# Weight blocks in one transfer each, and chunk 0 multiplied block by block

## The chip, the cores and the metric

The kernel runs on one core of a Trainium2 chip. The metric is the device time of one execution in microseconds (us); the time before is the median of three runs. A profile of one execution, with the time of every instruction and every DMA packet, goes with it. The engines are called PE (TensorE, the matrix products), DVE (VectorE), ACT (ScalarE), POOL (GpSimd) and SP (SyncE, which here issues stores); PEld is the loading of weights into TensorE.

## The reference

```python
# x: 16 x 512 x 1024, weight: 1024 x 768, both float32
y = np.matmul(x, weight)
mean = np.mean(y, axis=(0, 1), keepdims=True)
var = np.var(y, axis=(0, 1), keepdims=True)
y_norm = (y - mean) / np.sqrt(var + eps)
return (gamma * y_norm + beta).astype(np.float32)
```

A product of 8192 x 1024 with 1024 x 768, and a normalization of each of the 768 columns over all 8192 rows. No element of the output can be written before the last row of its column has been multiplied.

## The kernel before

**Tiles.** The 8192 rows of x are cut into 16 chunks of 512 rows. The 1024 elements of the inner dimension are cut into 4 blocks (`JW = 4`, index `jw`) of 256; each block is two steps (`e` = 0, 1) of 128, the partitions of TensorE. The 768 columns are six tiles of 128. Columns 0 to 255 (`NA`) are computed as rows (output rows on the partitions; `rows_unit`, `mm_rows`, line 493), the four tiles from column 256 on as columns (output columns on the partitions; `col_unit`, `mm`, line 558).

**Loads.** Both x and w are read as float32 and turned to bfloat16 by the DMA, all on GpSimd's queue. `w_sb` holds w as 128 partitions x 4 blocks x 2 x 768. Partition 32 i + c holds, for block jw, the two rows 2 (32 (4 i + jw) + c) and the next, 1536 elements that lie together in memory. One call of `load_w(jw, jw1)` (line 378) loads the blocks from jw up to jw1, in four transfers of 32 partitions, one for each i. `load_x` (line 386) also makes four transfers of 32 partitions. The order of the loads (line 426) is: x0 (rows 0 to 255 of chunk 0), block 0 of w, x1 (the other half of chunk 0), block 1, blocks 2 and 3 together, x2 and x3 (the halves of chunk 1), then chunks 2, 3 and on (line 392 issues all of x, line 383 all of w). VectorE turns each half chunk so that the inner dimension comes on the partitions (`turn_x`; line 421, for chunks 2, 3 and 6 line 414).

**The queue's lanes.** A transfer on GpSimd's queue gets one of eight semaphores in turn, so the issue of a transfer waits until the one eight places ahead of it has landed. The planner knows this as `LANES = 8`.

**The order of the work.** Every piece of work is a `Task` with a priority, a planned duration on one or several engines, and what it depends on. `arrange` is a planner that runs when the kernel is built: it takes again and again the engine that can begin first, and gives it the task of best priority among those that can begin within 0.2 us (`LOOK`) of the earliest. Its model of the DMA (`Wires`) uses fixed rates. The order that comes out is kept on each engine; on the chip, an engine that waits for something keeps everything behind it waiting. The turns of x have the best priority on VectorE (-1000 and up).

**Chunk 0 on TensorE.** Idle matmuls (`wake`, 16 on a zero tile and 22 small ones; lines 574 and 577) fill the time up to the arrival of data. Then come, by `part(q0, q1, jws)`: the first half of chunk 0 with block 0, a filler of four idle matmuls (`FILL`, 2 of `wake`), the second half with block 0, both halves with block 1. Then both halves with blocks 2 and 3: the rows (two units), and the four column tiles. Each of the six results of chunk 0 gathers in its own PSUM bank over all four blocks. When the rows of a half are done, ScalarE squares them (line 642), VectorE adds them to the running sums (line 645), GpSimd or VectorE adds the squares (line 649), and ScalarE keeps a copy (line 655). When a column tile is done, VectorE takes its statistics (line 694) and ScalarE keeps a copy (line 698). Chunk 1 begins after that, in two halves, with x2 and x3.

The rest of the kernel multiplies the other chunks, takes the statistics of one group of columns after the other, and normalizes, turns and stores a group while the next is multiplied.

Of the kernel before, what the change touches and what calls it, by code (L numbers as in the profile page):

```python
# [227 lines left out]
def kernel(  # L228
# [9 lines left out]
    nc = tc.nc  # L238
# [10 lines left out]
    NT = N // P  # L249
# [14 lines left out]
    GA = 2  # L264
# [26 lines left out]
    def seq(bi):  # L291

        ins = bi.ins
        prev = last.get(ins.engine)
        if prev is not None:
            tc.add_manual_dep(
                ins, prev,
                mybir.DependencyInfo(mybir.DependencyClass.NoSync, mybir.DependencyReason.DATA),
                reason="order",
            )  # L300
        last[ins.engine] = ins.name
        return bi
# [48 lines left out]
    def task(prio, engines, emit, deps=(), lock=False, **kw):  # L351
        t = Task(prio, engines, emit, deps, **kw)
        t.lock = lock
        tasks.append(t)
        return t

    def dve(occ):
        return {"DVE": (occ, occ + 0.09)}

    def act(occ):  # L360
        return {"ACT": (occ, occ + 0.11)}
# [14 lines left out]
    w_ready, x_ready, x_slot, plain, last_loads = {}, {}, {}, {}, []  # L376

    def load_w(jw, jw1):
        def emit(eng):
            rows = weight.rearrange("(i jw c e) n -> i c jw (e n)", i=4, jw=JW, e=2)  # L380
            dst = w_sb.rearrange("p jw e n -> p jw (e n)")
            for i in range(4):
                seq(nc.gpsimd.dma_start(dst[32 * i:32 * i + 32, jw:jw1], rows[i, :, jw:jw1]))
        return emit

    def load_x(m0, rows, slot):
        def emit(eng):
            x_bf = piece(slot).bitcast(bf16).rearrange("p (t k) -> p t k", k=KQ)
            slot.tile = x_bf
            src = x_flat[m0:m0 + rows].rearrange("(t r) k -> r t k", r=32)  # L390
            for i in range(4):
                bi = seq(nc.gpsimd.dma_start(x_bf[32 * i:32 * i + 32], src[:, :, KQ * i:KQ * (i + 1)]))  # L392
            slot.loader.ins = bi.ins
        return emit
# [8 lines left out]
    def turn_x(xslot, slot, m0, t0, jw0, jw1, new, rows=QR):  # L403
        def emit(eng):
            single = m0 // CH in SINGLE
            if new:
                xT_sb = xtpool.tile([P, JW, 2, CH] if single else [P, JW, CH, 2], bf16, tag="xT")
                slot.tile = xT_sb
            half, row = divmod((m0 + 32 * t0) % CH, QR)
            if single:  # L410
                src = xslot.tile[:, t0:t0 + rows // 32].rearrange("p t (jw c e) -> p t jw e c", jw=JW, e=2)
                dst = slot.tile[:, :, :, half * QR + row:half * QR + row + rows]
                dst = dst.rearrange("p jw e (t r) -> p t jw e r", r=32)
                seq(nc.vector.transpose(dst[:, :, jw0:jw1], src[:, :, jw0:jw1]))  # L414
                return
            src = xslot.tile[:, t0:t0 + rows // 32].rearrange("p t k -> p (t k)").bitcast(f32)
            src = src.rearrange("p (t jw c) -> p t jw c", jw=JW, c=32)
            dst = slot.tile.rearrange("p jw m e -> p (jw m e)").bitcast(f32)
            dst = dst.rearrange("p (jw q t r) -> p q t jw r", jw=JW, q=QPC, r=32)
            dst = dst[:, half, row // 32:(row + rows) // 32, jw0:jw1]  # L420
            seq(nc.vector.transpose(dst, src[:, :, jw0:jw1]))  # L421
        return emit

    for c in range(C):
        x_slot[c] = Slot(xts)
    order = [("x", 0), ("w", 0, 1)] + [("x", 1), ("w", 1, 2), ("w", 2, 4)]
    order += [("x", q) for q in range(2, SHORT * QPC)] + [("c", c) for c in range(SHORT, C - 1)]
    at = M - CH
    for rows in (CH-P,P):
# [2 lines left out]
    t = 1.0  # L432
    affine = None
    for kind, n, *n1 in order:
        if kind == "w":
            took = 4 * 192 * 4 * (n1[0] - n) / 4 * PER_KB * 1.024
            w_ready[n] = task(t, {"POOL": (2.0, 2.0)}, load_w(n, *n1), dma=took)
            w_ready[n].count = 4
            t += 2.1 * (n1[0] - n)
            if n1[0] == JW:  # L440
                idt = task(t, {"POOL": (0.6, 0.6)}, lambda eng: make_identity(nc, ident))
                task(t, act(0.25), lambda eng: seq(nc.scalar.copy(ident32, ident)), [idt])
            continue
        rows = n1[0] if kind == "p" else QR if kind == "x" else CH
        m0 = n if kind == "p" else n * rows
        if m0 == M // 2:
            affine = task(t, {"SP": (5.0, 7.0)}, load_affine, [x_ready[m0 // CH - 3, 0, JW]])
        slot = Slot(rings, rows // 32 * KQ // 2)
        load = task(
            t, {"POOL": (2.68 * rows / CH, 2.68 * rows / CH)}, load_x(m0, rows, slot), dma=rows * K * 4 / 1024 * PER_KB * 1.024,  # L450
            takes=[slot])
        load.count = 4
        slot.loader = load
        last_loads.append(load)
        t += 2.7 * rows / QR
        for i in range(rows // QR):
            c, q = divmod(m0 // QR + i, QPC)
            for j0, j1 in ((0, JW // 2), (JW // 2, JW)) if m0 < CH else ((0, JW),):
                new = q == 0 and j0 == 0
                x_ready[c, q, j1] = task(  # L460
                    -1000 + t, dve((2.2 if c in SINGLE else 1.16) * (j1 - j0) / JW + 0.02),
                    turn_x(slot, x_slot[c], m0, i * QR // 32, j0, j1, new), [load],
                    uses=[slot] if new else [slot, x_slot[c]], takes=[x_slot[c]] if new else [])
                if not new:
                    x_ready[c, q, j1].deps.append(x_ready[c, 0, JW // 2 if m0 < CH else JW])
            x_ready.setdefault((c, q, JW // 2), x_ready[c, q, JW])
        if rows % QR:
            t0 = rows // QR * QR // 32
            m1 = m0 + 32 * t0
            c, q = divmod(m1 // QR, QPC)  # L470
            x_ready["tile", m1 // P] = task(
                -1000 + t, dve(0.63), turn_x(slot, x_slot[c], m0, t0, 0, JW, False, P),
                [load, x_ready[c, 0, JW]], uses=[slot, x_slot[c]])
            x_ready[c, q, JW] = x_ready[c, q, JW // 2] = x_ready["tile", m1 // P]
# [123 lines left out]
    def rows_unit(c, ts, jws=range(JW)):  # L598
        key = "row", c, ts[0]
        slot = bank_of.setdefault(key, None) or Slot(banks)  # L600
        bank_of[key] = slot
        kw = {"takes": [slot], "uses": [x_slot[c]]} if jws[0] == 0 else {"uses": [slot, x_slot[c]]}
        h = ts[0] * P // QR
        t = pe_task(0.873 * len(ts) * len(jws) / JW, mm_rows(c, ts, list(jws), slot),
                    waits(jws, c, h, h + 1), key, **kw)
        if jws[-1] == JW - 1:
            rows_stats(c, ts, slot, t)
        return t

    def col_unit(nt, c, jws, q0=0, q1=QPC):  # L610
        slot = bank_of.setdefault((nt, c), None) or Slot(banks)
        bank_of[nt, c] = slot
        first = jws[0] == 0 and q0 == 0
        xs = [plain[c][0][jw] for jw in jws] if c in plain else [x_slot[c]]
        kw = {"takes": [slot], "uses": xs} if first else {"uses": [slot] + xs}
        t = pe_task((1.728 if c in plain or c in SINGLE else 1.808) * len(jws) / JW * (q1 - q0) / QPC,
                    mm(nt, c, list(jws), slot, q0, q1),
                    waits(jws, c, q0, q1) + ([plain[c][1][jw] for jw in jws] if c in plain else []), (nt, c), **kw)
        if q1 - q0 == QPC:
            t.hosts = 4  # L620
        if jws[-1] == JW - 1 and q1 == QPC:
            col_stats(nt, c, slot, t)
        return t
# [133 lines left out]
    def part(q0, q1, jws):  # L757
        for h in range(q0, q1):
            rows_unit(0, [2 * h, 2 * h + 1], jws)
        for nt in range(GA, NT):  # L760
            col_unit(nt, 0, jws, q0, q1)
# [3 lines left out]
    pe_task(0.87 * FILL, wake(FILL, fill_slot), [w_ready[0]], takes=[fill_slot])  # L765
    part(1, 2, [0])
    part(0, 2, [1])
    for h in range(2):
        rows_unit(0, [2 * h, 2 * h + 1], [2, 3])
    for nt in range(GA, NT):  # L770
        col_unit(nt, 0, [2, 3])

    halves = [range(JW // 2), range(JW // 2, JW)]
    merges = []
# [455 lines left out]
    nt = NT - 1  # L1230
# [40 lines left out]
    for c, r0, rows in ends:  # L1271
        due = E + 2.0 + 0.6 * c
        n = max(rows // CH, 1)
# [30 lines left out]
    order = arrange(tasks, turns)  # L1304
# [39 lines left out]
```

## Time and profile before

| | |
|---|---|
| median of 3 runs | 207.76 us (207.47 to 208.3) |
| span of the profiled execution, first to last instruction | 206.5 us |
| time of the profiled execution itself | not given by the page; the median is 1.26 us above the span |
| TensorE busy | 191.4 us, 93% of the span |
| VectorE, ScalarE, GpSimd busy | 76%, 68%, 64% |
| granted clock of TensorE, mean | 0.985 of full speed |
| DMA moved | 48.73 MB, of which 18.36 MB by GpSimd's queue |
| issue of one transfer of w on GpSimd | 0.51 us, 12 of them |

How to read it: times in the views are counted from the start of the span. A line of a timeline gives start, length, engine, source line, operation, what is written and what is read, and how many instructions are drawn together; in brackets stands how long the engine had been idle and what released it. A line of the waits gives who waited for whom, the sum in us, the number of waits and the longest. A line of a table of windows gives the stretch, its length, the busy time of PE, PEld, DVE, ACT and POOL, the granted clock, the DMA engines' share, and GB/s (counted in bytes written, so that a load that halves its bytes counts half). The DMA issues give KB of each transfer and the median time from issue to landing.

### The profile page before, as it was taken

Reading aid. Unit: us, or ns where it says so; the run is one execution under the profiler, and the core shown is the slowest. Engines: PE = TensorE matmul, PEld = TensorE weight load, DVE = VectorE, ACT = ScalarE, POOL = GpSimd, SP = SyncE. Lnnn points to the kernel's source line nnn. Section 1 sums busy time; section 2 is a strip of 40 time slices with the busy share of each in tenths; the row PEclk is TensorE's granted clock in tenths of the full one; section 3 lists DMA queues with packets and bytes.
Section 4 is the critical chain, followed back from the end, with each engine's and each line's share of the span. In section 5 each row is a group of like instructions: output and inputs, shape, how many; then the busy total and the mean of one; then the engine's idle time right before and its main releaser. Section 6 shows DMA issues by size and latency. Waiting matters only on the chain.

```text
span 206.5 us, 3506 instructions
## 1 busy us (share of the span) xinstructions
PE 191.4 (93%) x1211; PEld 116.3 (56%) x1226; DVE 156.3 (76%) x238; ACT 139.8 (68%) x248; POOL 132.0 (64%) x148
## 2 busy tenths in 40 slices
PE   7998999999999999999999999999999999996900
PEld 3465564747488888777875444444444445553600
DVE  4220779999999999968989998977999648947900
ACT  2000560369989999998978767997376776866950
POOL 7877964877488999999304999599954440440000
PEclk9999999999999999999999999999999999999995
DMA  5999999999999999999676898999999999999898
GB/s 55 169 168 193 192 196 196 196 198 197 190 193 197 197 197 195 196 197 195 110 120 199 311 339 307 267 350 307 315 317 245 291 325 308 274 341 347 254 347 243
DMA packets 98497, 48.73 MB, mean 236 GB/s; under 512 B 24240, under 2 KB 97968, under 8 KB 98480
## 3 DMA queue, kind: packets, MB, share of 16 engines
q0 software_dynamic: 34688, 18.36, 65.1%
q1 hardware_dynamic: 63792, 30.16, 52.8%
q8 instruction: 9, 0.15, 0.3%
q14 instruction: 8, 0.07, 0.1%
HBM read 36.71 MB, written 25.17 MB: 300 GB/s over the span
## 4 chain that ended last, share of the span: by engine, by line
PE 82%; DMA 8%; ACT 3%; issue 1%; POOL 1%; DVE 1%; ACTq 0%; POOLq 0%
PE y_ps L558 51%; PE y_ps L493 23%; DMA ring<-in_x_dram 5%; PE y_ps L798 4%; ACT o_sb L1293 3%; DMA w_sb<-in_weight_dram 3%; PE o_ps L1028 2%; PE a_ps L887 1%; POOL ring L392 1%; PE y_ps L736 1%; PE o_ps L1058 0%; ACTq L1339 0%; PE tot_ps L855 0%; DVE fin L743 0%; ACT y_sb L746 0%
## 5 line engine op out<-in xcount | busy, mean ns | idle before, releaser
L558 PEld LDWEIGHTS <-w_sb 128*128 128x128 bf16 x512 | 49.7, 97 | 57.4
L558 PE MATMUL y_ps<-x_pl,w_sb 128*128 128x512 bf16 x256 | 60.5, 379 | 0.3
L392 POOL DMA_DIRECT2D ring<-in_x_dram x76 | 47.5, 630 | 13.0 <-DVE xT_sb L414 5.0
L558 PE MATMUL y_ps<-xT_sb,w_sb 128*128 128x512 bf16 (+1 forms) x241 | 55.1, 376 | 0.4
L493 PE MATMUL y_ps<-w_sb,xT_sb 128*128 128x256 bf16 x448 | 50.7, 273 | 0.6 <-DMA w_sb<-in_weight_dram 0.6
L493 PEld LDWEIGHTS <-xT_sb 128*128 128x128 bf16 x448 | 43.6, 98 | 8.3 <-issue 1.7
L421 DVE STREAM_TRANSPOSE xT_sb<-ring 128x1024 f32<-128x1024 f32 (+1 forms) x29 | 31.2, 1111 | 12.4 <-DMA ring<-in_x_dram 12.2
L694 DVE BATCH_NORM_STATS2 stats<-y_ps 128x6 f32<-128x512 f32 x46 | 30.9, 687 | 12.7 <-PE y_ps L558 12.5
L698 ACT CAST y_sb<-y_ps 128x512 bf16<-128x512 f32 x51 | 29.4, 590 | 14.5 <-DVE stats L694 12.4
L926 POOL TENSOR_TENSOR ring<-ring,sum 128x1024 f32<-128x1024 f32 (+1 forms) x11 | 23.7, 2193 | 14.6 <-DVE ring L921 14.5
L649 POOL TENSOR_TENSOR sum<-sum,sq_sb 128x512 f32<-128x512 f32 x21 | 26.9, 1281 | 3.2 <-ACT sq_sb L642 2.1
L642 ACT ACTIVATE sq_sb<-y_ps 128x512 f32<-128x512 f32 x28 | 16.3, 607 | 18.0 <-PE y_ps L493 17.1
L645 DVE TENSOR_TENSOR sum<-y_ps,sum 128x512 f32<-128x512 f32 x28 | 18.9, 675 | 9.1 <-ACT sq_sb L642 7.8
L530 ACT COPY x_pl<-xT_sb 128x1024 bf16<-128x1024 bf16 x24 | 24.4, 1052 | 1.7 <-DVE xT_sb L421 1.7
L655 ACT CAST y_sb<-y_ps 128x512 bf16<-128x512 f32 x28 | 16.0, 599 | 7.8 <-DVE sum L645 7.6
L530 POOL COPY x_pl<-xT_sb 128x1024 bf16<-128x1024 bf16 x15 | 16.1, 1108 | 8.0 <-DVE x_pl L530 5.2
L921 DVE TENSOR_TENSOR ring<-y_sb,a_ps 128x1024 f32<-128x1024 bf16 (+1 forms) x16 | 16.7, 1080 | 0.3 <-DMA out_dram<-ring 0.3
L1139 POOL TENSOR_TENSOR ring<-ring,sum 128x1024 f32<-128x1024 f32 x4 | 9.6, 2412 | 11.0 <-DVE ring L1135 11.0
L1193 ACT CAST ring<-ring 128x1024 f32<-128x1024 bf16 x15 | 15.7, 1049 | 1.0 <-DMA ring<-y_sb 1.0
L1028 PE MATMUL o_ps<-ident,y_sb 128*128 128x128 bf16 x104 | 14.2, 221 | 2.2 <-DVE y_sb L1280 2.0
L414 DVE STREAM_TRANSPOSE xT_sb<-ring 128x2048 bf16<-128x2048 bf16 x6 | 13.5, 2289 | 0.2 <-DMA ring<-in_x_dram 0.2
L574 PE MATMUL idle_ps<-idle_sb 128*128 128x512 f32 x20 | 11.2, 717 | 1.5 <-DVE idle_sb L314 1.5
(97 smaller groups left out, 155.0 us busy)
## 6 DMA issues: line engine op xcount, KB each, us to landing
out_dram<-ring SPq DMA_DIRECT2D x38, 512.0 KB, 3.7
ring<-in_x_dram POOLq DMA_DIRECT2D x52, 256.0 KB, 8.8
out_dram<-o_sb SPq DMA_DIRECT2D x6, 512.0 KB, 4.9
ring<-in_x_dram POOLq DMA_DIRECT2D x16, 128.0 KB, 5.3
out_dram<-ring SPq DMA_DIRECT2D x4, 256.0 KB, 3.0
w_sb<-in_weight_dram POOLq DMA_DIRECT2D x8, 96.0 KB, 5.1
w_sb<-in_weight_dram POOLq DMA_DIRECT2D x4, 192.0 KB, 5.9
ring<-in_x_dram POOLq DMA_DIRECT2D x4, 192.0 KB, 8.1
```

The source lines that it names most:

```text
L392: bi = seq(nc.gpsimd.dma_start(x_bf[32 * i:32 * i + 32], src[:, :, KQ * i:KQ * (i + 1)]))
L421: seq(nc.vector.transpose(dst, src[:, :, jw0:jw1]))
L493: seq(nc.tensor.matmul(y_ps[:, s], x_of(c, jw, e, t * P, (t + 1) * P), w_sb[:, jw, e, 0:NA], start=(s == 0 and jw == 0 and e == 0), stop=( ...
L530: seq(nc.scalar.copy(dst, pairs) if eng == "ACT" else ENG[eng].tensor_copy(dst, pairs))
L558: seq(nc.tensor.matmul(y_ps, w_sb[:, jw, e, nt * P:(nt + 1) * P], moving(c, jw, e, q0 * QR, q1 * QR, parted), start=(jw == 0 and e == 0 an ...
L645: seq(nc.vector.tensor_add(sum1, slot.tile[:, 0:n], sum1))
L649: seq(ENG[eng].tensor_add(acc, acc, state["sq"][:, 0:n]))
L694: seq(nc.vector.bn_stats(dst, slot.tile))
L698: seq(nc.scalar.copy(y(nt, c), slot.tile))
L921: seq(nc.vector.tensor_mul(slot.o, y_row[c].y[:, s0:s1], aff[0][:, None, :].to_broadcast([P, n, NA])))
L926: seq(ENG[eng].tensor_add(slot.o, slot.o, row[:, None, :].to_broadcast([P, n, NA])))
L1028: seq(nc.tensor.transpose(dst, src, ident))
```

## The change

`load_w` makes one transfer for each block over all 128 partitions, instead of four for 32 partitions each. Blocks 2 and 3 are loaded and waited for one by one, and chunk 0 is multiplied first by block 2 and then by block 3, by the same `part` that does block 1, instead of by both in each unit. The planner's figures for GpSimd's time of a load of w and for the number of its transfers change with that: 0.6 us and one transfer for each block, instead of 2.0 us and four for each call.

```diff
 def load_w(jw, jw1):
     def emit(eng):
         rows = weight.rearrange("(i jw c e) n -> i c jw (e n)", i=4, jw=JW, e=2)
         dst = w_sb.rearrange("p jw e n -> p jw (e n)")
-        for i in range(4):
-            seq(nc.gpsimd.dma_start(dst[32 * i:32 * i + 32, jw:jw1], rows[i, :, jw:jw1]))
+        for j in range(jw, jw1):
+            seq(nc.gpsimd.dma_start(dst[:, j], rows[:, :, j]))
     return emit
...
-order = [("x", 0), ("w", 0, 1)] + [("x", 1), ("w", 1, 2), ("w", 2, 4)]
+order = [("x", 0), ("w", 0, 1)] + [("x", 1), ("w", 1, 2), ("w", 2, 3), ("w", 3, 4)]
...
-        w_ready[n] = task(t, {"POOL": (2.0, 2.0)}, load_w(n, *n1), dma=took)
-        w_ready[n].count = 4
+        w_ready[n] = task(t, {"POOL": (0.6 * (n1[0] - n), 0.6 * (n1[0] - n))}, load_w(n, *n1), dma=took)
+        w_ready[n].count = n1[0] - n
...
 part(0, 2, [1])
-for h in range(2):
-    rows_unit(0, [2 * h, 2 * h + 1], [2, 3])
-for nt in range(GA, NT):
-    col_unit(nt, 0, [2, 3])
+part(0, 2, [2])
+part(0, 2, [3])
```

## The prediction

> **What bounds the kernel now.** I read the page's busy shares first, then who waited for whom on TensorE, then the chain that ended last, then the timelines of the first 30 us.
>
> ```profile
> PE 191.4 (93%) x1211; PEld 116.3 (56%) x1226; DVE 156.3 (76%) x238; ACT 139.8 (68%) x248; POOL 132.0 (64%) x148
> ...
> w_sb<-in_weight_dram POOLq DMA_DIRECT2D x8, 96.0 KB, 5.1
> w_sb<-in_weight_dram POOLq DMA_DIRECT2D x4, 192.0 KB, 5.9
> ```
> ```profile
> PE o_ps L1028 <- DVE y_sb L1280: 2.0, 1, 2.0
> PE idle_ps L574 <- DVE idle_sb L314: 1.5, 1, 1.5
> PE y_ps L493 <- DMA w_sb<-in_weight_dram: 0.6, 1, 0.6
> ```
> TensorE is busy 93% of the span and waits three times in all: at the start, in the tail, and once for w. So each microsecond by which the matmuls begin later, or stand still before about 188 us, comes out at the end.
>
> ```profile
> 8.65 4.67 DMA ring<-in_x_dram
> 13.32 0.28 issue
> 13.61 6.00 DMA w_sb<-in_weight_dram
> 19.61 0.14 issue
> 19.74 1.91 PE y_ps L493 x16
> 21.65 3.62 PE y_ps L558 x16
> 25.26 3.67 PE y_ps L493 x32
> ```
> The chain (start, length): the last transfer of w is issued at 13.61, lands at 19.61 and ends the 0.6 us wait; chunk 0 ends at 25.26.
>
> ```profile
> 3.73 1.99 POOL L383 DMA_DIRECT2D w_sb<-in_weight_dram  x4
> ...
> 10.83 1.22 PE L577 MATMUL idle_ps<-idle_sb 128*128 128x128 bf16 x19
> 11.89 0.60 PE L493 MATMUL y_ps<-w_sb,xT_sb 128*128 128x256 bf16 x4
> ...
> 13.24 1.88 PE L574 MATMUL idle_ps<-idle_sb 128*128 128x512 f32 x4
> 14.96 0.60 PE L493 MATMUL y_ps<-w_sb,xT_sb 128*128 128x256 bf16 x4
> ...
> 21.44 0.69 DVE L645 TENSOR_TENSOR sum<-y_ps,sum 128x512 f32<-128x512 f32 x1 [6.69 <-ACT sq_sb L642]
> 22.05 0.68 DVE L649 TENSOR_TENSOR sum<-sum,sq_sb 128x512 f32<-128x512 f32 x1
> 22.65 1.24 DVE L421 STREAM_TRANSPOSE xT_sb<-ring 128x1024 f32<-128x1024 f32 x1
> ```
> TensorE fills its time to 12.06 with idle matmuls; the first real one follows without a gap, so block 0 of w and the first half of chunk 0 are there by then. The page lists no execution time beside its 206.5 us span; the median of the runs, 207.76, is 1.26 above it, and I add my sum to that median.
>
> **GpSimd issues.** Twelve transfers of 0.51 us become four. At 0.5 to 0.6 us each this frees some 4 us of GpSimd before 14 us, where TensorE does not depend on it: worth nothing by itself. A transfer here waits for the eighth before it on its queue (the fourth transfer of x1 starts as one of x0 lands, 7.94). With fewer ahead, blocks 1, 2 and 3 can be issued near 8.6 to 10 instead of 9.22 to 13.61. The identity, built on GpSimd at 5.70, moves behind x1's issues and costs nothing: nobody turns a block with it before 100 us. Behind a late block on that queue wait, by the same rule of eight, the issues of x2 (its first for block 0, the others for x1) and x3 (for x1 and blocks 1 to 3).
>
> **How wide one transfer runs.** This is the unknown. Before, each w transfer has 32 rows as its outermost count on both sides. Its replacement reads a source of 4 x 32 rows, outermost count 4: within a group the rows of w lie 2 apart, 32 of them make 64 rows, but the next group begins 256 rows on, so the two counts can't be drawn into one of 128. No row of this profile shows such a transfer. The packet records give each 3,072-byte row 0.248 us on its engine, and sixteen such rows at a time; the same by bandwidth:
>
> ```profile
> 16.00:19.00 3.00, 2.94 (x20) 1.70 (x18) 0.00 (x0) 0.00 (x0) 2.18 (x5) 1.00 1.11 199
> ```
> (The last number is GB/s.) A block is 4 x 96 KB = 393 kB: 2.0 us at 199 GB/s on sixteen engines, 7.9 us on four (32 rows x 0.248). These are my two ends; a block can't get faster than 2.0, since all sixteen were already full. I take four: the count 4 is the only thing about the transfer that differs from the rows shown, and a transfer dealt out by its outermost count has four shares. The rows shown would look alike if inner rows were dealt out too, so sixteen stays a rival.
>
> [...]
>
> **The sum with four engines.** Block 0's packets began before at 6.0 and most of them after 7.0, behind x0's. Begun at 7.2, 7.9 us long, 0.3 to be counted as landed: 15.5 instead of before 11.9. The idle matmuls still end at 12.06, so TensorE stands 3.4 us. Then quarter-chunk products of 1.4 and the second idle filler of 1.9 end at 18.7. On these four engines x1 lies behind block 0: 15.2 + 2.7 (524 kB at 195 GB/s) = 17.9, landed 18.2, and the first half of its transpose, 0.7, ends near 18.95. The products of x1 start there, not at 14.96, and everything queued behind them on TensorE moves with them: **+4.0**. Blocks 1 to 3, if each goes to four other engines (if not, rival 3), lie there behind x1's share, done near 10, and end near 18 to 18.6. Block 1 is wanted at 20.3, block 2 at 23.1, block 3 at 25.9: no wait, and the old 0.6 goes: **-0.6**.
>
> **What the split of blocks 2 and 3 does to VectorE.** The row sums of chunk 0 now finish after block 3 instead of before the column products. VectorE's order is laid down at build time by the planner's constants. Worked by hand, half 0's sum is ready there at 21.79 and the transpose of x2 at 22.00; a task of better priority goes first only within 0.2 us, so the sum goes first by 0.009. The order is then sum, x2 transpose, sum, one bn_stats, x3 transpose. (The same reckoning gives the order seen before.) On the chip, counted from the start of block 2's products: half 0 done at 3.24 (0.95 + 1.81 + 0.48), its square starts 0.1 later, the sum 0.63 after that (21.44 - 20.81), the x2 transpose 0.61 later and 1.24 long: 5.82. TensorE ends chunk 0 at 5.52: it stands 0.35. Then sum, bn_stats (0.6 each) and the x3 transpose end at 8.2, while TensorE wants it at 5.87 + 1.83 = 7.7: 0.6 with the weight load. Together **+0.95**; if a little of the order falls otherwise, between 0 and 1.1. x2, issued from 15.5 to 18.2, and x3, from 18.2 on (before: up to 20.5, ready at 25.71), land near 21 and 24, before their transposes at 27.7 and 30, so this is no DMA wait. The squares and copies on ScalarE and the PSUM banks have 1 us or more to spare; behind the x3 transpose only bn_stats are queued. After chunk 1 the matmuls run as before: their loads come no later than they did.
>
> +4.0 - 0.6 + 0.95 = +4.35: **212.1 us**.
>
> **The clock.** It can add to this: the standstill is 3.4 us.
>
> ```profile
> 190.00:207.00 17.00, 5.46 (x64) 3.61 (x64) 5.87 (x20) 7.71 (x11) 0.00 (x0) 0.81 0.92 278
> ```
> The trace's clock record falls to 0.5 in the tail; a mean of 0.81 over the last 17 us means that for 6.5 us, thus from 200.5, 4.1 us after the last matmul. So 3.4 should pass; if not, some 1.7 us or more is lost, which sets the upper end. [...]
>
> **The rivals.** (1) Sixteen engines, VectorE's order as above: -0.6 + 0.95 = +0.35, 208.1. For it: the full rate in every row; against it: outermost count 4. (2) Not slower: sixteen engines and the transposes of x2 and x3 not held up, so that only the 0.6 goes: 207.2, decided by block 0 landing before 12.06 and the x2 transpose ending before TensorE leaves chunk 0. Against it the 0.009. (3) All four blocks on the same four engines: block 3 lands near 7.2 + 4 x 7.9 = 39, chunk 0 ends near 42 instead of 25.26: 225. Nothing in the rows excludes it.
>
> **How the numbers follow.** Four engines in rotation 0.78 (of its own 210.8 to 214.2, the top being the clock); rival 1 0.11; rival 2 0.07; rival 3 0.04. A measurement here tells about 0.5% from no change, 206.72 to 208.80. Rivals 1 and 2 lie mostly inside: 0.15; faster by more 0.03; slower 0.82. The range takes in rival 1 and the clock: 207.8 to 214.2, leaving out rivals 2 and 3 and the tails.
>
> **What would show it.** Right: w transfers landing 8 to 11 us after issue at a lower GB/s per transfer; the first L493 matmul near 15.5 behind a DMA wait of 3 us or more; no wait for w near 23; short waits at the start of chunk 1 on L421. Wrong: the first matmul still at 11.9. Then the width was misjudged and the time is that of rivals 1 or 2. If the first matmul is late and the rest is not, the x1 or VectorE term was.

## The result, and the profile after

The changed kernel takes 215.97 us (median of 6 runs, 213.91 to 217.28) against 208.04 us (6 runs, 207.47 to 208.91) for the kernel before: a ratio of 1.0354 with a 95% interval of 1.0317 to 1.039. It is slower, as forecast, but by 7.9 us instead of 4.35, and above the range, which ended at 214.2. Its runs lie further apart than those of before.

The profiled execution has a span of 214.7 us, 8.2 more than before. The page of the kernel after (busy times; the granted clock in 40 slices of 5.4 us, 9 being full speed; the issues of w with KB and median us to landing; packets, MB and share of GpSimd's queue):

```profile
PE 194.9 (91%) x1211; PEld 119.0 (55%) x1226; DVE 156.8 (73%) x237; ACT 139.3 (65%) x248; POOL 129.5 (60%) x141
...
PEclk9995899999999999999999999999999999999685
...
q0 software_dynamic: 36096, 18.36, 66.9%
...
w_sb<-in_weight_dram POOLq DMA_DIRECT2D x4, 384.0 KB, 15.7
```

TensorE has the same 1211 instructions and is busy 3.5 us longer: there is a dip of the clock in the fourth and fifth slice (tenths 5 and 8; before has 9 in both). A block of w lands 15.7 us after its issue, where a transfer of 32 partitions took 5.1. The queue moves the same bytes in 1,408 more packets (34,688 before).

Who waited for whom on TensorE, after (us in total, times, longest):

```profile
PE y_ps L493 <- DMA w_sb<-in_weight_dram: 5.1, 1, 5.1
...
PE y_ps L493 <- DVE xT_sb L421: 0.7, 2, 0.4
```

One wait for w, now at the first block; the 0.6 us wait for the last block is gone, and two short waits for the transposes of x2 and x3 are new. The rest of the delay is no wait. The chain that ended last, after (start, length):

```profile
3.72 13.48 DMA w_sb<-in_weight_dram
17.24 1.01 PE y_ps L493 x4
18.25 1.71 PE y_ps L558 x8
19.96 3.39 PE idle_ps L574 x4
23.35 0.57 PE y_ps L493 x4
```

The first products start at 17.24 instead of 11.89 and take 1.0 us where the same products take 0.6 at full speed (the clock record reads 0.5 from 16.36 to 23.19); the four idle matmuls that fill the time before x1 take 3.4 us instead of 1.88; the products of x1 start at 23.3 instead of 14.96. VectorE's timeline, after, shows that x1 was no earlier than this (in brackets: idle before, and what ended it):

```profile
22.53 1.30 DVE L421 STREAM_TRANSPOSE xT_sb<-ring 128x512 f32<-128x512 f32 x2 [12.95 <-DMA ring<-in_x_dram]
31.28 0.69 DVE L645 TENSOR_TENSOR sum<-y_ps,sum 128x512 f32<-128x512 f32 x1 [7.44 <-ACT sq_sb L642]
31.89 1.23 DVE L421 STREAM_TRANSPOSE xT_sb<-ring 128x1024 f32<-128x1024 f32 x1
33.05 0.65 DVE L645 TENSOR_TENSOR sum<-y_ps,sum 128x512 f32<-128x512 f32 x1
33.62 0.68 DVE L694 BATCH_NORM_STATS2 sums<-y_ps 128x6 f32<-128x512 f32 x1
34.23 1.22 DVE L421 STREAM_TRANSPOSE xT_sb<-ring 128x1024 f32<-128x1024 f32 x1
```

x1 is turned at 22.53, so two things end within 0.2 us of each other: the filler at half clock (23.35) and the first half of x1's turn (23.2). The second to sixth line are the order that the forecast worked out by hand: sum, turn of x2, sum, one bn_stats, turn of x3. Windows after (stretch, length, busy PE, PEld, DVE, ACT, POOL, clock, DMA share, GB/s):

```profile
12.00:16.00 4.00, 0.14 (x3) 0.02 (x1) 0.00 (x0) 0.00 (x0) 0.00 (x0) 1.00 1.20 169
16.00:20.00 4.00, 2.76 (x13) 2.01 (x13) 0.00 (x0) 0.00 (x0) 1.80 (x4) 0.54 1.37 150
20.00:24.00 4.00, 4.00 (x11) 1.37 (x11) 1.30 (x2) 0.00 (x0) 1.43 (x3) 0.60 1.67 108
```

From 16 to 24 us the DMA moves 150 and 108 GB/s, where before moved 195 in both windows:

```profile
16.00:20.00 4.00, 3.34 (x23) 1.97 (x22) 0.00 (x0) 0.00 (x0) 2.81 (x6) 1.00 1.18 195
20.00:24.00 4.00, 4.00 (x28) 2.40 (x26) 2.56 (x4) 1.67 (x3) 3.78 (x6) 1.00 1.44 195
```

So the transfers do not follow one another at the rate of before; the steps below show how they lie.

**The sum of the delay, read from the trace.** The second part of chunk 0 (the products of x1) is 8.34 us later, the old wait is gone (-0.6) and the turns add 0.7: +8.4, beside +8.2 in the span. The same three numbers account for the span of nearly every experiment below, so each is told by them.

**What each block's semaphore shows.** In the trace a transfer on GpSimd's queue counts 16 steps as it lands, as many as the page has DMA engines. Of block 0, twelve steps are counted by 7.9 us and the last four at 16.7 to 17.2; from 8 to 11 us the packet records have 4.3 rows of 3,072 bytes under way at once (in before, from 13 to 15 us, 16.3). I read this as four engines that move the block and twelve that have nothing of it; the records don't name a packet's engine. Blocks 1, 2 and 3 end at 23.41, 23.72 and 24.02, side by side. x1's four transfers end at 18.06, 18.92, 19.69 and, the last one, 22.51, each with twelve early steps (by 9.6 to 12.8) and four late ones.

### The profile page after: what moved, and what is told of

Read it like the earlier page. It is cut to its first block, busy times and chain, and to the rows that moved or that the text cites. A ratio compares the mean times of both kernels' runs of the same rounds, so it can differ in the third digit from the quotient of the medians.

```text
span 214.7 us, 3489 instructions
## 1 busy us (share of the span) xinstructions
PE 194.9 (91%) x1211; PEld 119.0 (55%) x1226; DVE 156.8 (73%) x237; ACT 139.3 (65%) x248; POOL 129.5 (60%) x141
## 4 chain that ended last, share of the span: by engine, by line
PE 82%; DMA 6%; ACT 3%; issue 2%; DVE 2%; POOL 1%; ACTq 0%; DVEq 0%; POOLq 0%
PE y_ps L558 50%; PE y_ps L493 22%; DMA w_sb<-in_weight_dram 6%; PE y_ps L796 3%; ACT o_sb L1291 2%; PE o_ps L1026 2%; PE idle_ps L574 2%; POOL ring L392 1%; PE y_ps L736 1%; PE a_ps L885 1%; DVE xT_sb L421 1%; ACTq L1337 0%; PE o_ps L1056 0%; PE tot_ps L853 0%; DVE sum L645 0%
## 5 line engine op out<-in xcount | busy, mean ns | idle before, releaser
L392 POOL DMA_DIRECT2D ring<-in_x_dram x76 | 47.3, 629 | 23.2 <-DMA w_sb<-in_weight_dram 8.6
L493 PE MATMUL y_ps<-w_sb,xT_sb 128*128 128x256 bf16 x448 | 51.3, 274 | 5.8 <-DMA w_sb<-in_weight_dram 5.1
L558 PE MATMUL y_ps<-xT_sb,w_sb 128*128 128x512 bf16 (+1 forms) x241 | 56.0, 381 | 0.4
L698 ACT CAST y_sb<-y_ps 128x512 bf16<-128x512 f32 x51 | 29.5, 591 | 14.0 <-DVE stats L694 13.2
L642 ACT ACTIVATE sq_sb<-y_ps 128x512 f32<-128x512 f32 x28 | 16.9, 613 | 27.5 <-PE y_ps L493 27.2
L924 POOL TENSOR_TENSOR ring<-ring,sum 128x1024 f32<-128x1024 f32 (+1 forms) x11 | 23.7, 2183 | 15.4 <-ACT ring L1064 11.6
L530 POOL COPY x_pl<-xT_sb 128x1024 bf16<-128x1024 bf16 x16 | 17.1, 1105 | 6.7 <-DVE x_pl L530 4.0
L655 ACT CAST y_sb<-y_ps 128x512 bf16<-128x512 f32 x28 | 15.4, 603 | 6.4 <-DVE sum L645 6.4
L1191 ACT CAST ring<-ring 128x1024 f32<-128x1024 bf16 x15 | 15.8, 1050 | 1.4 <-DMA ring<-y_sb 1.4
L1026 PE MATMUL o_ps<-ident,y_sb 128*128 128x128 bf16 x104 | 13.6, 248 | 2.2 <-DVE y_sb L1278 2.0
L574 PE MATMUL idle_ps<-idle_sb 128*128 128x512 f32 x20 | 13.0, 814 | 1.5 <-DVE idle_sb L314 1.5
## 6 DMA issues: line engine op xcount, KB each, us to landing
w_sb<-in_weight_dram POOLq DMA_DIRECT2D x4, 384.0 KB, 15.7
```

Of the source, the lines that this page charges most:

```text
L493: seq(nc.tensor.matmul(y_ps[:, s], x_of(c, jw, e, t * P, (t + 1) * P), w_sb[:, jw, e, 0:NA], start=(s == 0 and jw == 0 and e == 0), stop=( ...
L530: seq(nc.scalar.copy(dst, pairs) if eng == "ACT" else ENG[eng].tensor_copy(dst, pairs))
L558: seq(nc.tensor.matmul(y_ps, w_sb[:, jw, e, nt * P:(nt + 1) * P], moving(c, jw, e, q0 * QR, q1 * QR, parted), start=(jw == 0 and e == 0 an ...
L574: seq(nc.tensor.matmul(idle_ps, idle_sb[:, 0:P], idle_sb, start=True, stop=True))
L698: seq(nc.scalar.copy(y(nt, c), slot.tile))
L924: seq(ENG[eng].tensor_add(slot.o, slot.o, row[:, None, :].to_broadcast([P, n, NA])))
```

## The experiments

Every kernel is the one after with the edit shown. "Second part" is the start of the products of x1 with block 0.

### Is it the transfers or the order of the products?

**e1: four transfers for each block again, the new order kept.**

```diff
-            for j in range(jw, jw1):
-                seq(nc.gpsimd.dma_start(dst[:, j], rows[:, :, j]))
+            for i in range(4):
+                seq(nc.gpsimd.dma_start(dst[32 * i:32 * i + 32, jw:jw1], rows[i, :, jw:jw1]))
```

The planner's two figures for a load of w are those of before again.

> The change without its narrow transfers: each block of w again in four transfers of 32 partitions, blocks 2 and 3 loaded and waited for apart, chunk 0 multiplied by each as in the changed kernel. Theory 'few engines' (the loss comes from transfers of w that run on four engines): blocks land as before, the first real matmul follows the idle ones near 11.9, the wait of 0.6 us for w is gone or shorter, and VectorE's new order costs up to 0.95 at the start of chunk 1: between 207.4 and 208.6 beside 208.0 before, ratio 0.997 to 1.003. Rival 'order' (the loss comes from the new order of products and from what the planner makes of it): near the changed kernel, 214 to 216, ratio about 1.03.

209.58 us, 1.0059 [1.0034, 1.0084], a little above the expected range; span 207.3. No wait for w is left, and the second part starts at 14.17. What it loses it loses at chunk 1, with 2.0 us of waiting for the turns of x2 and x3. x2 itself comes later (VectorE stands 0.51 us for it and 0.59 for x3), for its issues begin at 15.56 instead of 14.67: sixteen transfers of w now stand on the queue before it where twelve stood, and each issue waits for the eighth before it (in before x1's third transfer begins at 7.94, 0.28 us after the third of x0 has landed, at 7.66, and the first issue of x2 at 14.67, 0.28 us after the eighth before it has landed, at 14.39; in after at 17.49, 0.29 us after block 0, the eighth before it there, at 17.20). -0.8 - 0.6 + 2.0 = +0.6, beside +0.8 in the span.

**e2: one transfer for each block, the old order of the products.**

```diff
-    part(0, 2, [2])
-    part(0, 2, [3])
+    for h in range(2):
+        rows_unit(0, [2 * h, 2 * h + 1], [2, 3])
+    for nt in range(GA, NT):
+        col_unit(nt, 0, [2, 3])
```

> The other part alone: one transfer for each block of w as in the changed kernel, but chunk 0 multiplied by blocks 2 and 3 together as before. 'Few engines': block 0 lands near 17.2 and x1 near 22.5 as in the changed kernel; VectorE's short waits at the start of chunk 1 (0.7 us in the changed kernel) go, nothing else: 215, ratio 1.030 to 1.036. Rival 'order': near 208.0, ratio about 1.00.

216.47 us, 1.0361 [1.0302, 1.0419]: the whole loss without the new order. The wait for block 0 is 6.0 us here. The loss lies in the transfers.

### Is it the size of the transfer or its shape?

**e3: one transfer of 128 partitions from 256 consecutive rows of w,** so that 128 is the outermost count.

```diff
-                seq(nc.gpsimd.dma_start(dst[:, j], rows[:, :, j]))
+                src = weight[256 * j:256 * j + 256].rearrange("(p e) n -> p (e n)", e=2)
+                seq(nc.gpsimd.dma_start(dst[:, j], src))
```

> The changed kernel, still with one transfer for each block over all 128 partitions, but each reads 256 consecutive rows of w, so that the source has an outermost count of 128 (w then lies in wrong rows: the product is not the reference's; times are). 'Few engines by the outermost count': sixteen engines again, block 0 lands by 10, first matmul at 11.9, 207.4 to 208.6, ratio 0.997 to 1.003. Rival 'one large transfer is slow in itself' (its size, its one issue, its 128 partitions): block 0 near 17, 214 to 216, ratio 1.03.

208.29 us, 0.9997 [0.9972, 1.0022]. Of e3, the issues of w and two lines of TensorE's timeline:

```profile
w_sb<-in_weight_dram POOLq DMA_DIRECT2D x4, 384.0 KB, 8.3
```
```profile
10.94 1.39 PE L578 MATMUL idle_ps<-idle_sb 128*128 128x128 bf16 x22
12.16 0.60 PE L494 MATMUL y_ps<-w_sb,xT_sb 128*128 128x256 bf16 x4
```

The same bytes in the same number of transfers land after 8.3 us instead of 15.7, block 0 at 10.0, and TensorE does not stand still. Here one large transfer cost nothing (208.29 us beside 208.42 before); the shape of its source did (215.97).

**e4 and e5: eight groups of 16 rows, and two groups of 64.** The new lines are those of e4; e5 has 2 groups, 401 rows apart.

```diff
+                src = weight[23 * j:23 * j + 8 * 119].rearrange("(i r) n -> i r n", i=8)
+                src = src[:, 0:32].rearrange("i (c e) n -> i c (e n)", e=2)
+                seq(nc.gpsimd.dma_start(dst[:, j], src))
```

> The changed kernel, each block read as eight groups of 16 rows, 119 rows apart (the product is not the reference's). 'Engines by the outermost count': eight engines, 16 rows of 0.25 us each, block 0 lands near 12.0 to 13, first matmul near 12.1 to 13, the time 208.5 to 211. Rival 'any transfer that isn't one even run of 128 rows falls back to four engines or to one fixed number': block 0 near 17, 214 to 217.

> The changed kernel, each block read as two groups of 64 rows, 401 rows apart (the product is not the reference's). 'Engines by the outermost count': two engines, 64 rows of 0.25 us each, block 0 lands near 23 to 25 and x1 behind it near 26 to 30, the time 219 to 228. Rival 'a fixed number of four': 214 to 217.

One run each: 209.78 us (span 208.0) and 222.13 us (span 220.4). Block 0 of e4 has eight steps by 8.5 us and the other eight at 11.6 to 13.2; that of e5 has fourteen by 7.8 and two at 22.50 and 23.48. TensorE's timeline of e5:

```profile
23.52 1.01 PE L494 MATMUL y_ps<-w_sb,xT_sb 128*128 128x256 bf16 x4 [12.23 <-DMA w_sb<-in_weight_dram]
```

| outermost count of the source | 128 (e3) | 8 (e4) | 4 (after) | 2 (e5) |
|---|---|---|---|---|
| last step of block 0, us | 10.0 | 13.2 | 17.2 | 23.5 |

In these four kernels the late steps of block 0 follow the outermost count: eight in e4, four in after, two in e5, and in e3 all sixteen by 10.0 us. I read their number as that of the engines that move it.

### Why is the second part 8.3 us later, and not 4.0?

**e6: the four groups 199 rows apart and the blocks 67,** so that engines don't read at like distances.

```diff
+                src = weight[67 * j:67 * j + 4 * 199].rearrange("(i r) n -> i r n", i=4)
+                src = src[:, 0:64].rearrange("i (c e) n -> i c (e n)", e=2)
+                seq(nc.gpsimd.dma_start(dst[:, j], src))
```

> The changed kernel with the same four groups of 32 rows in each transfer, but the groups begin 199 rows apart instead of 256, and the blocks 67 instead of 64, so that the sixteen engines no longer read rows a multiple of 192 KB apart (the product is not the reference's). Theory 'reads collide' (rows slow down from 0.248 to 0.34 to 0.40 us because the engines read in step at that distance): rows stay near 0.25, block 0 lands near 15.3, x1 near 18.2, 211 to 213, ratio 1.015 to 1.025. Rival 'writes collide' (groups and blocks write the same few partitions in step) or any cause that isn't the source's distance: row times and landings as in the changed kernel, 214 to 216, ratio 1.03.

216.27 us, 1.0382 [1.034, 1.0424]. In the packet records of after, a row of 3,072 bytes takes 0.33 to 0.40 us from 13 us on (medians of each microsecond); here it takes 0.248, as before the change, until about 15.7, and 0.27 to 0.31 later. But block 0 still ends at 16.92 and x1 at 21.35, and no time is won. Nor is it shown that the rows differ by the distance: e15 below, with the same odd distances, has 0.30 to 0.38 from 13 us on, and the profile of e12, with the distances of after, has 0.25 to 0.27 until 19 us.

**e7: only block 0 in one transfer,** blocks 1 to 3 in four (for these the planner has 2.0 us and four transfers).

```diff
+            if jw == 0:
+                seq(nc.gpsimd.dma_start(dst[:, jw], rows[:, :, jw]))
+            else:
+                for i in range(4):
+                    seq(nc.gpsimd.dma_start(dst[32 * i:32 * i + 32, jw], rows[i, :, jw]))
```

> The changed kernel with one transfer for block 0 of w only; blocks 1 to 3 in four transfers of 32 partitions each. Theory 'crowding' (with all four blocks narrow the rows slow down, and the last quarter of x1 is counted late, 2.8 us after the third, behind what the later narrow blocks leave on the same engines): block 0 still lands near 16.5, but the quarters of x1 follow at 0.8 us each and the last lands by 20.5 instead of 22.5. The time stays at 213.5 to 215.5, since with the clock at half the filler ends only near 22.5. Rival 'block 0 alone does it all': x1 lands near 22.5 as in the changed kernel, 215 to 216.5.

215.58 us, 1.0347 [1.0293, 1.04]. Block 0 ends at 15.86 and x1 at 18.56, with its four transfers 0.7 us apart and no laggard: without the three other blocks as narrow transfers, x1 is nearly as early as forecast (18.2). But little else lies beside it here: GpSimd issues the fourth transfer of block 1, and all behind it, only from 16.14 on, 0.28 us after block 0 has landed; block 0 is the eighth transfer before it. The second part still starts only at 20.53, since the clock was at half from 15.8 to 19.2. What is won there is lost at chunk 1, which waits 2.2 us for x2 and x3: they stand behind twelve transfers of w instead of three. So this kernel tells of x1, but by its time alone it would have told nothing.

**e13: block 0 as in after, blocks 1 to 3 as in e3,** which keeps four transfers of w.

```diff
+                flat = weight[256 * j:256 * j + 256].rearrange("(p e) n -> p (e n)", e=2)
+                seq(nc.gpsimd.dma_start(dst[:, j], flat if j else rows[:, :, j]))
```

> The changed kernel with only block 0 read as four groups; blocks 1 to 3 are one transfer each of 256 consecutive rows (the product is not the reference's), so that there are as few transfers as in the changed kernel but one narrow one. 'Crowding': block 0 lands near 15.9, x1 near 18.6; the clock falls near 16 and the filler ends near 20.5, so the second part starts there, 5.5 later than before; less 0.6 for w and plus 0.7 on VectorE: ratio 1.022 to 1.030. Rival 'block 0 alone does it all': 1.032 or more.

**e14: e13 with eight more idle matmuls ahead of the first product,** not told to the planner, so that every order stays. (`wake` makes two for each count.)

```diff
-            for _ in range(count):
+            for _ in range(count + (4 if count == WAKE else 0)):
```

> The kernel with only block 0 narrow and 8 more idle matmuls that the planner is not told of (they end near 15.5): neither crowding nor the slow clock. This is the case that the forecast's sum described: second part near 19.4 (+4.4), -0.6 for w, +0.7 on VectorE: +4.5, ratio 1.018 to 1.025. If it is above 1.030, the sum lacked something else.

e13: 214.71 us, 1.0317 [1.0271, 1.0363], above the range expected for 'crowding' and just short of the rival's 1.032: block 0 landed at 17.17 and not near 15.9, so the time does not decide here, and the landing of x1 does (19.29, 2.1 us after block 0). e14: 213.08 us, 1.023 [1.0186, 1.0275], as expected. TensorE's timelines of e13 and of e14:

```profile
17.22 1.01 PE L494 MATMUL y_ps<-w_sb,xT_sb 128*128 128x256 bf16 x4 [5.02 <-DMA w_sb<-in_weight_dram]
...
19.73 1.96 PE L575 MATMUL idle_ps<-idle_sb 128*128 128x512 f32 x4
21.53 0.60 PE L494 MATMUL y_ps<-w_sb,xT_sb 128*128 128x256 bf16 x4
```
```profile
16.70 0.60 PE L494 MATMUL y_ps<-w_sb,xT_sb 128*128 128x256 bf16 x4 [1.49 <-DMA w_sb<-in_weight_dram]
...
18.04 1.88 PE L575 MATMUL idle_ps<-idle_sb 128*128 128x512 f32 x4
19.75 0.60 PE L494 MATMUL y_ps<-w_sb,xT_sb 128*128 128x256 bf16 x4
```

In both, x1 has landed by 19.3 and TensorE does not wait for it. In e13 the clock is at half from 16.48 to 19.90; in e14 it stays full. Of the 1.78 us between the two second parts, 0.52 is block 0's own landing and 1.26 the clock. With the clock kept and the other blocks wide, the forecast's construction gives its time: +4.8 for the second part, -0.6, +0.7 = +4.9, and the span is +4.9.

### Can the clock alone be given back to the changed kernel?

**e9: `WAKE` 14 instead of 8, the planner told; e11: e7 with `WAKE` 13.**

> The changed kernel with 28 instead of 16 idle matmuls at the start (they end near 17.2 instead of 12.06), so that TensorE's clock has no long idle stretch in which to fall to half (16.4 to 23.2 in the changed kernel). Theory 'x1 ends last': the second half of chunk 0 isn't turned before 23.2 in any case, and the slow clock only filled time in which TensorE would have waited: no gain, 1.030 to 1.040. Rival 'the clock': products and filler at full speed win 2.5 us or so: 1.020 to 1.027.

> The kernel with one transfer for block 0 only, and 26 instead of 16 idle matmuls (end near 16.4), so that neither crowding nor the clock counts. If the forecast's sum was right but for these two and for block 0's slowest engine (landing 16.5 instead of 15.5): second part of chunk 0 near 20.0 to 20.5, 212.5 to 213.8, ratio 1.021 to 1.027. If crowding and clock were not what the forecast lacked: as the changed kernel, 1.03 or more.

e9: 216.9 us, 1.0354 [1.0309, 1.04]. e11: 217.2 us, 1.0408 [1.036, 1.0456], a miss of the expected 1.021 to 1.027. In both the planner, told of the idle matmuls, also laid later work in another order (TensorE gets new short waits, such as 1.0 us for GpSimd in e11), so their times don't isolate the clock. In e9 the first products do start at 16.96 at full speed, and TensorE then stands 2.59 us for x1.

**e12, e15, e16: idle matmuls that the planner isn't told of,** as in e14: 12 more in the changed kernel (e12), 12 in e6 (e15), 14 in the changed kernel (e16).

> The changed kernel with 12 more idle matmuls at the start, which the planner is not told of, so that the order of everything else stays as it is (in the run with 28 idle matmuls in the plan it moved). They end near 17.2, and the clock should not fall before chunk 0 is through. 'x1 ends last': the second half of chunk 0 is turned near 23.2 as before, the time stays at 1.030 to 1.038. 'The clock': 1.018 to 1.027.

> The changed kernel with groups 199 and blocks 67 rows apart (the product is not the reference's) and 12 more idle matmuls that the planner is not told of. If crowding is the engines reading in step at multiples of 192 KB, it is gone here, and with the clock kept the ratio is that of one narrow block, 1.019 to 1.027. If it has another cause (writes to the same partitions, the small packets that a narrow transfer leaves on the engines that it doesn't use), x1 still lands near 21 to 22.5 and the ratio is 1.030 or more.

> The changed kernel with 14 more idle matmuls that the planner is not told of (they end near 17.9; 12 more gave 1.035 with an interval too wide to tell, 214.2 to 221.6 us). With block 0 alone narrow the kept clock brought 1.0317 to 1.023. 'Crowding holds x1 back': with all four blocks narrow most executions still wait for x1, the ratio stays at 1.030 or above, and above 1.0275 with its whole interval. 'The clock is all that the forecast lacked': 1.020 to 1.027.

e12: 218.17 us, 1.0347 [1.0253, 1.0441], its four runs between 214.15 and 221.62. e15: 218.71 us, 1.0485 [1.0433, 1.0538]. e16: 219.05 us, 1.0492 [1.0441, 1.0542]; its profiled execution took 553 us and is not read. Keeping TensorE busy gave the changed kernel no time back: e15 and e16 are slower than the same kernels without the idle matmuls (e6 and after), and e12, by its interval, can't be told from after. The two profiles show two different courses. That of e12 is of its fastest run, 214.15 us; TensorE's timeline:

```profile
18.17 1.88 PE L574 MATMUL idle_ps<-idle_sb 128*128 128x512 f32 x4
20.09 0.61 PE L493 MATMUL y_ps<-w_sb,xT_sb 128*128 128x256 bf16 x4
```

All four blocks are narrow here too, yet x1 lands at 19.30, 3.1 us after block 0 (16.21), the rows stay at 0.25 to 0.27 us until 19 us, and TensorE does not wait for x1. So narrow blocks do not hold x1 back in every execution. The profile of e15, TensorE's timeline:

```profile
18.26 1.88 PE L575 MATMUL idle_ps<-idle_sb 128*128 128x512 f32 x4
22.49 1.03 PE L494 MATMUL y_ps<-w_sb,xT_sb 128*128 128x256 bf16 x4 [2.35 <-DVE xT_sb L422]
23.32 1.91 PE L559 MATMUL y_ps<-xT_sb,w_sb 128*128 128x256 bf16 x8
```

The first standstill is covered, but x1 comes as late as in e6 (21.70), although the distances are odd, so there is a second one, and the trace's clock record falls to half at 22.27 for 3.41 us. In after the half speed lay over the filler, where it cost little, and had passed by the time the products of x1 began (the record returns to full at 23.19). Here it lies over those products: at half speed from 22.49 to 25.68 they lose 1.6 us of what 0.8 us of earlier start had won. So the second half of chunk 1 starts at 36.20 instead of 35.50. That 0.7 is half of the 1.4 us by which this span exceeds that of after (216.1 to 214.7); the other half comes in the tail, and is not explained.

### The spans, from three numbers of each trace

| kernel | second part | later by | waits for turns at chunk 1 | sum with -0.6 | span, us more than before |
|---|---|---|---|---|---|
| before | 14.96 | | 0 | | 206.5 |
| after | 23.30 | 8.3 | 0.7 | 8.4 | 8.2 |
| e4, eight | 16.50 | 1.5 | 0.7 | 1.6 | 1.5 |
| e6, odd pitch | 22.48 | 7.5 | 0.7 | 7.6 | 7.4 |
| e7, only block 0 | 20.53 | 5.6 | 2.2 | 7.2 | 7.0 |
| e13, block 0 alone | 21.53 | 6.6 | 0.7 | 6.7 | 6.6 |
| e14, with idle matmuls | 19.75 | 4.8 | 0.7 | 4.9 | 4.9 |
| e12, fastest run | 20.09 | 5.1 | 0.7 | 5.2 | 5.6 |

## Why the prediction was right in its mechanism and wrong in its size

**Right: four engines in rotation.** The step that took "four" for the outermost count is borne out by the steps of block 0 (four late ones) and by e4 and e5 (eight and two), and by e3, where block 0 has landed by 10.0. That the engines change from block to block was my estimate, which no row of before shows. In after, blocks 1 to 3 end within 0.6 us of each other near 24 and not one behind the other, so rival 3 is out; of their sixteen steps eight, twelve and sixteen come after 22.5 us, four more with each block, as four other engines for each would give.

**Right by luck: no wait for blocks 1 to 3.** They landed at 23.4 to 24.0, where the forecast had 18 to 18.6. Block 1 was wanted only at 24.66, because all before it was late; at the forecast's 20.3 TensorE would have waited for it.

**Right: the small terms.** The old wait for w is gone (-0.6). VectorE's order is the one worked by hand, and costs 0.32 + 0.40 = 0.7 instead of 0.95. TensorE stood for the turn of x3 0.40 us, not 0.6.

**Mis-sized: block 0's landing, 15.5 forecast, 17.2 measured.** The forecast let the block begin at 7.2 on all its engines, with 32 rows of 0.248 behind each other. In the packet records of after, its rows run in number only from between 7.6 and 7.9 us on (one begins at 6.54), and from 13 us on a row takes 0.33 to 0.40. In e7, where the rows of block 0 stay near 0.25, its last step comes at 15.9, 0.4 after the forecast. So some 0.4 of the 1.7 is the later begin, and the rest goes with the slow rows here. Slow rows are not the only cause of a late step: in e14 the rows take 0.248 throughout, and the last step still comes at 16.7; why is not known.

**Mis-sized: x1 behind block 0, 2.7 us forecast, 5.3 measured** (17.2 to 22.5). The forecast priced x1 at the full 195 GB/s, as if blocks 1 to 3 didn't matter to it. With those blocks read as in e3 (e13: 19.29) or issued later (e7: 18.56) x1 ends 2.1 and 2.7 us after block 0, the forecast's size. With all four narrow, the last transfer of x1 in after ends 2.8 us after the third. But how late x1 comes differs from execution to execution and goes with the rows: 3.1 us after block 0 in e12 (rows of 0.25 to 0.27 us), 4.4 in e6 (0.27 to 0.31), 4.8 in e15 (0.30 to 0.38), 5.1 in e9 (0.33 to 0.42), 5.3 in after (0.33 to 0.40), 6.3 in e2 (0.40 to 0.49). So four narrow blocks side by side can hold x1 back, and do in five of these six profiles; what slows the rows in one execution and not in another isn't shown. The distances of the reads alone don't decide it (e12 and e15).

**Failed: the clock, "so 3.4 should pass".** The standstill was 5.1 us, and the clock fell at 16.36, 4.2 us after the last idle matmul, for 6.83 us. But the row that I read (a fall 4.1 us after the last matmul in the tail) gave no threshold of 4.1: in the profile of e15 the clock fell 2.1 us into a standstill. In the clock records of these runs, the stretches at full and at half speed within the kernel last multiples of 3.41 us: 10.24, 6.83, 177.49 and twice 3.41 in after, 194.56 in before. Counted by how much of each such period TensorE is without a matmul (the ends of matmuls are modelled in a profile, so hundredths should not be leaned on): from full speed, periods with up to 1.8 us of idling were followed by full speed (1.82 in the tail of e12, 1.80 in that of e3), those with 1.9 us or more by half speed (1.93 in the tail of after, 2.1 at the second standstill of e15). From half speed, 0.7 us of idling in a period was followed by full speed (e13), 0.9 by another period at half (after). In after the standstill took one whole period, from 12.95 to 16.36. An estimate from these counts: of the 3.4 us that I forecast, at least 1.7 falls into one period of 3.41 wherever the periods lie, and the clock would have stayed up only if a period's end cut the standstill near its middle, so passing was the less likely case.

**Why the upper end was too low.** I added the clock as 1.7 us or more, an estimate that no run shows, on top of a landing that I held to be certain. Landing (+1.7), half speed (+2.9 between 17.24 and 23.30, where the forecast had 3.2 for the products and the filler), and x1 (+4.3) were all wider than the term allowed. They don't add: the filler and x1 end together at 23.2 to 23.35, so removing either alone wins next to nothing: in e6 x1 lands at 21.35 and the filler holds TensorE until 22.48, in e9 and e15 the clock is kept and x1 is late. Only e14, which removes both, and the fastest run of e12, where neither occurs, come near the forecast's time (213.08 and 214.15, forecast 212.1).

**The base.** The profiled execution of after takes 216.47 us for its span of 214.7, 1.77 outside it, where I had taken 1.26 from the median. By median to median it does not matter: 207.76 + 8.2 = 215.96, and 215.97 was measured.

**Open:** what slows the rows and x1 in most executions when all four blocks are narrow; the scatter of such kernels (after 213.9 to 217.3 us, e12 214.2 to 221.6), where the six runs of before lie within 1.5 us; and whether the second standstill that the profile of e15 shows is the reason in e12's slower runs and in e16 too, whose profiles don't show it.

## What to carry to other kernels

Look at the pattern of a merged transfer's source as well as at the destination's 128 partitions: here merging was free with an outermost count of 128 (e3, 208.29 us beside 208.42), and not with 8, 4 and 2 (209.78, 215.97 and 222.13 us). When a transfer gets narrow, price it and what lies behind it by the last step to be counted, and not at the rate that the rows had before (block 0 landed at 17.2 and x1 at 22.5, where that rate gave 15.5 and 18.2). Price a standstill of TensorE by how much of it can fall into one period of the clock record (3.41 us here; 1.8 us of idling in one was followed by full speed, 1.9 by half). And where a wait and a slow clock end together, test with both removed: here e14, which removes both, took 213.08 us, e13, which leaves the clock at half, 214.71, and e15, which leaves x1 late, 218.71.

## What the runs showed of the hardware that was not expected

- The kernels with narrow transfers have more packets of 4 bytes on GpSimd's queue (2,816 in after, 1,408 in before). By the pages' packets under 512 bytes, e3 has 24,112; e13 has 384 more, e4 512, after 1,536 and e5 3,584. By number this is the early steps of block 0, times the rows of 3,072 bytes for each late one, times the narrow blocks: 12 x 32 x 1, 8 x 16 x 4, 12 x 32 x 4 and 14 x 64 x 4. Before, with 8 transfers more than e3, has 128 more than e3, 16 for each, which gives the 1,408 more packets of the page of after.
- The issue of a transfer of w over 128 partitions on GpSimd took 0.53 to 0.60 us in e3 (outermost count 128), 0.58 to 0.62 in e4 (8), 0.67 to 0.71 in after (4) and 0.80 to 0.83 in e5 (2); one over 32 partitions took 0.49 to 0.54 in before.
- With four narrow blocks side by side, rows of 3,072 bytes slowed from 0.248 to 0.33 to 0.40 us in after, up to 0.49 in e2, and only to 0.25 to 0.27 until 19 us in the profiled run of e12, at the same distances.
- In the clock records of these runs TensorE's clock fell at the end of a period of 3.41 us with 1.9 us or more without a matmul (1.93 in the tail of after), and not after one with 1.8 us or less (1.82 in the tail of e12).
